# Six pairs of column blocks of an input projection as seven half products each, on token-major operands, with weights loaded two k tiles at a time

## The chip, the core and the metric

The kernel runs on one core of a Trainium2 chip. The metric is the device time of one execution in microseconds (us). TensorE (PE in the profile) does the matrix products, VectorE (DVE) and ScalarE (ACT) the elementwise work, GpSimd (POOL) small powers and the DMAs of its own queue; SyncE (SP) issues most other DMAs. Every engine takes its instructions in the order in which they stand in its queue.

## The reference, cut to what matters

Two layers, 512 tokens, width 2048. `w_in` has 6720 columns:

```python
hn = rms_norm(h, attn_norm[i])
proj = hn @ w_in[i]
(a_u, a_v, a_z, b_b, b_c, b_h, b_z, c_q, c_kv, c_kr, c_z) = jnp.split(proj, split_pts, axis=-1)
y_a = spatial_gating(a_u, a_v, a_z, ...)      # 3 x 512 columns
y_b = short_conv(b_b, b_c, b_h, b_z, ...)     # 4 x 512 columns; c * h goes through a 3-tap conv
y_c = latent_attention(c_q, c_kv, c_kr, c_z)  # 8 x 192, 512, 64, 1024 columns
h = h + concat(rms_norm(y_a), rms_norm(y_b), rms_norm(y_c)) @ w_out[i]
gate = sigmoid(rms_norm(h, ple_norm[i]) @ w_ple_gate[i])
h = h + gate * (p[i] @ w_ple_proj[i])
```

## The kernel before

All arithmetic is fp32, made of fp32r products. `split` cuts a tile into `hi` (a cast on ACT) and `lo` (source minus `hi`, on DVE), and `mm3` makes three matmuls of each product: hi by hi, hi by lo, lo by hi. Activations are split once and stay on the chip (`splitU`, tiles of the pool `big`); weights come 256 KB at a time: `weight` has SP load a tile `raw` of 128x512 (5 buffers), ACT writes `whi`, DVE writes `wlo` (6 buffers each). One such tile serves 12 matmuls.

`groupT` makes an output with features on partitions: the stationary operand is a 128x128 piece of the weight, the moving one 512 tokens of one k tile of x. `groupN` makes an output with tokens on partitions: the stationary operand is a 128x128 piece of x, the moving one a weight row of 384, 448 or 512 columns. `groupK` is `groupT` with k outermost. All walk the 16 k tiles of x (`xs`).

One layer: `groupK` for `ckv`; `groupT` for `za`, `groupN` for `v`, `groupT` for `u`, the spatial gate; then `c`, `h`, `zb`, `b` by `groupT` with the four query pairs (`queries`, `groupN`) between them; `normed` writes the finished halves of `y` to DRAM. Then attention over 8 heads: `kv` (256-column matmuls), `scores`, softmax, `weightsT` (transposes on PE), `values`. Between these, `fillers` gives PE pieces of independent work (12 matmuls each, counted by `ST` and `FN`): the 8 blocks of `zc`, then the first half of the output projection. At the end the second half of the output projection (`ev_out`) and the gate (`ev_gate`), with six PSUM banks in rotation (`TAGS`).

The framework orders each engine's instructions by the order of the code, by when its own estimate has the operands ready, and by free buffers; the program that results is fixed. Names: `raw`, `whi`, `wlo` are the weight tiles, `hi`, `lo` halves of activations, `mm`, `s`, `o`, `tr` PSUM banks, `rs` the result of `rpow` (a power on POOL), `rT` a row of per-token factors that goes through DRAM (`rd`).

Of the kernel before, what the change touches and what calls it, by code (L numbers as in the profile page):

```python
# [11 lines left out]
F32 = mybir.dt.float32  # L12
# [6 lines left out]
P = 128  # L19
# [24 lines left out]
FQ = 2 * (NOPE + ROPE)  # L44

# [22 lines left out]
NU, RAWB, HIB, SB = 62, 5, 6, 3  # L68

ST, FN = (4, 4, 4, 4, 4), (2, 1, 1, 1, 1)  # L70

FETCH = ((0, 1, 2, 3), (4, 5, 6, 7), (), ())
# [13 lines left out]
def trunk(ctx, tc, xT, pT, pos, freq, pars, rows, wsp, wckv, wv, w512, wq0, wq, wkv, wout, wgate, wple, outT):  # L86
# [6 lines left out]
    wst = ctx.enter_context(tc.tile_pool(name="wst", bufs=4))  # L93
    tmp = ctx.enter_context(tc.tile_pool(name="tmp", bufs=4))
# [13 lines left out]
    TMPS = {"t": 2, "n": 2, "q": 2, "z": 2, "o": 2, "q4": 3}  # L108

    def T(s, tag="t", dt=F32):  # L110
        return tmp.tile([P, S], dt, tag=tag, name=nm(s), bufs=TMPS[tag])

    NB = ("s", "s", "s", "o") if SB == 3 else ("s", "s", "tr", "o")
    BANKS = {"mm": 2, "s": SB, "o": 1, "tr": 5 - SB}
# [6 lines left out]

    ident = cst.tile([P, P], F32, name="ident")
    make_identity(nc, ident)
    ones = cst.tile([P, P], F32, name="ones")
# [9 lines left out]
    ydram = drp.tile([8, 2, P, S], F32, name="ydram")  # L134
    mdram = drp.tile([KD, P, S], F32, name="mdram")
    qdram = drp.tile([HEADS, P, S], F32, name="qdram")
    rdram = drp.tile([NPAIR, P, S], F32, name="rdram")
    zdram = drp.tile([HEADS, P, S], F32, name="zdram")
# [17 lines left out]
    def weight(src, n):  # L156
        raw = wst.tile([P, S], F32, tag="raw", name=nm("raw"), bufs=RAWB)
        sync.dma_start(raw[:, :n], src)
        hi = wst.tile([P, S], F32R, tag="whi", name=nm("whi"), bufs=HIB)
        lo = wst.tile([P, S], F32R, tag="wlo", name=nm("wlo"), bufs=HIB)  # L160
        split(raw[:, :n], None, hi[:, :n], lo[:, :n])
        return hi, lo

    def mm3(out, lh, ll, rh, rl, start, stop):
        pe.matmul(out, lh, rh, start=start, stop=False)  # L165
        pe.matmul(out, lh, rl, start=False, stop=False)  # L166
        pe.matmul(out, ll, rh, start=False, stop=stop)  # L167

    def groupT(srcs, xs, evac, tags=("mm",)):

        nq = len(xs) // 4
        for f in range(len(srcs)):
            ps = bank(tags[f % len(tags)])
            for q in range(nq):
                wh, wl = weight(srcs[f][q], S)
                for i in range(4):
                    c = slice(i * P, (i + 1) * P)
                    k = 4 * q + i
                    mm3(ps, wh[:, c], wl[:, c], xs[k][0], xs[k][1], k == 0, k == len(xs) - 1)
            evac(f, ps)  # L180

    def groupK(srcs, load, evac):

        pb = [bank(t) for t in NB]
        for i, src in enumerate(srcs):
            xh, xl = load(i)
            wh, wl = weight(src, S)
            for f in range(4):
                c = slice(f * P, (f + 1) * P)
                mm3(pb[f], wh[:, c], wl[:, c], xh, xl, i == 0, i == len(srcs) - 1)  # L190
        for f in range(4):
            evac(f, pb[f])

    def groupN(srcs, xs, n, evac):

        pb = [bank(t) for t in NB]
        for i, (src, (xh, xl)) in enumerate(zip(srcs, xs)):
            wh, wl = weight(src, n)
            for t in range(NT):
                c = slice(t * P, (t + 1) * P)  # L200
                mm3(pb[t][:, :n], xh[:, c], xl[:, c], wh[:, :n], wl[:, :n], i == 0, i == len(xs) - 1)
        for t in range(NT):
            evac(t, pb[t][:, :n])

    class Stat:


        def __init__(self, tag="q"):
            self.acc = None
            self.tag = tag  # L210

        def add(self, src):
            if self.acc is None:
                self.acc = tmp.tile([P, S], F32, tag="acc", name=nm("acc"), bufs=2)
                a.activation(out=self.acc, in_=src, func=AF.Square)
            else:
                sq = T("sq", self.tag)
                a.activation(out=sq, in_=src, func=AF.Square)
                v.tensor_tensor(out=self.acc, in0=self.acc, in1=sq, op=ALU.add)
# [10 lines left out]
    def rpow(m, n):  # L230
        r = small(n, "rs")
        g.tensor_tensor(out=r, in0=m, in1=mhalf[:, 0:n], op=ALU.pow)  # L232
        return r

# [7 lines left out]


    def tables():
# [24 lines left out]
        for unit, bits, n in ((2.0 ** 16, 9, 4), (2.0 ** 2, 11, 2)):  # L269
            piece = rnd(ang, unit, "piece")  # L270
# [4 lines left out]
            for c in cs + [rest]:  # L275
                q = w("q")
# [9 lines left out]
        v.tensor_tensor(out=turn, in0=turn, in1=r, op=ALU.subtract)  # L286

# [5 lines left out]
        for c in cs + [rest]:  # L293
            v.scalar_tensor_tensor(out=turn, in0=k, scalar=-8.0 * c, in1=turn, op0=ALU.mult, op1=ALU.add)
        lim = 3.1415925
# [8 lines left out]
        return cos, sin  # L304
# [37 lines left out]


    st = Stat()
    xs = []
    col = lambda i, c: par[:, i * NCOL + c:i * NCOL + c + 1]

    def load0(k):
        t = T("x")
        a.dma_start(t, xT[k])  # L350
        xs.append(splitU(t, col(0, C_ATTN + k)))
        st.add(t)
        return xs[k]

    cos = sin = None
# [519 lines left out]
```

## Time and profile before

| | before |
|---|---|
| time, median of 3 runs | 2198.72 us (2198.12 to 2202.12) |
| the profiled execution | 2199.84 us, its span 2198.1 us |
| PE busy in the span | 2180.6 us, 10720 matmuls |
| DVE, ACT, POOL busy | 1119.8, 905.0, 221.0 us |
| mean granted TensorE clock | 0.998 |

The profile is of one execution; its time lies 1.7 us above its span and 1.1 us above the median. A busy time of PE counts matmuls that overlap, so what one matmul costs is read as the distance between the starts of neighbours.

### The profile page before, as it was taken

What the parts mean: (1) busy time and instruction counts of PE and PEld (TensorE: products, weight loads), DVE (VectorE), ACT (ScalarE), POOL (GpSimd) and SP (SyncE); (2) the same over time, 40 slices, a digit from 0 to 9 for tenths busy, and PEclk for the clock granted to TensorE, in tenths of its full rate; (3) what the DMA queues carried; (4) which work ended last, traced back from release to release, by engine and by line L of the source; (5) the groups of instructions that cost most, each with busy time, mean ns of one, the idle gap of its engine ahead of it and who ended that gap; (6) DMA issues with size and microseconds to landing.
All of it is one profiled execution on the core that took longest, in us unless ns stands there. A gap on an engine that the chain in (4) does not pass through costs nothing.

```text
span 2198.1 us, 29729 instructions
## 1 busy us (share of the span) xinstructions
PE 2180.6 (99%) x10720; PEld 1872.6 (85%) x10720; DVE 1119.8 (51%) x2326; ACT 905.0 (41%) x1709; POOL 221.0 (10%) x333
## 2 busy tenths in 40 slices
PE   8999999999999999999999999999999999999999
PEld 7888888988888888888888888889888888888887
DVE  7444354436466656655533444444355566575433
ACT  6332233324576544443332323233246665443222
POOL 0000000002131101100000001000021221011000
PEclk9999999999999999999999999999999999999999
DMA  7333534435354444454333335333353644354432
GB/s 212 103 105 91 138 101 117 113 77 188 106 179 145 132 120 125 127 152 120 115 98 104 99 83 151 97 112 119 78 181 109 187 135 135 111 144 136 124 117 70
DMA packets 142740, 272.22 MB, mean 124 GB/s; under 512 B 17329, under 2 KB 34113, under 8 KB 142593
## 3 DMA queue, kind: packets, MB, share of 16 engines
q1 hardware_dynamic: 122256, 214.83, 34.2%
q0 software_dynamic: 18032, 51.30, 7.7%
q10 hardware_dynamic: 2304, 4.20, 0.7%
q8 instruction: 84, 1.38, 0.3%
q14 instruction: 64, 0.52, 0.1%
HBM read 234.58 MB, written 35.67 MB: 123 GB/s over the span
## 4 chain that ended last, share of the span: by engine, by line
PE 74%; DMA 2%; issue 1%; DVE 1%; POOL 0%; ACT 0%; DVEq 0%; ACTq 0%; POOLq 0%
PE mm L165 13%; PE mm L166 13%; PE mm L167 13%; PE s L167 6%; PE s L165 6%; PE s L166 6%; PE o L166 2%; PE o L167 2%; PE o L165 2%; PE tr L639 1%; PE tr L340 1%; PE tr L166 1%; PE tr L167 1%; PE tr L165 1%; PE s L615 1%
## 5 line engine op out<-in xcount | busy, mean ns | idle before, releaser
L145 DVE TENSOR_TENSOR wlo<-raw,whi 128x512 fp32r<-128x512 f32 (+2 forms) x754 | 502.6, 670 | 619.6 <-ACT whi L144 602.5
L144 ACT CAST whi<-raw 128x512 fp32r<-128x512 f32 (+2 forms) x754 | 449.1, 603 | 847.0 <-PE mm L166 426.4
L165 PE MATMUL mm<-hi,whi 128*128 128x512 f32 x1312 | 512.7, 391 | 1.1 <-DVE pt L387 1.0
L166 PE MATMUL mm<-lo,whi 128*128 128x512 f32 x1312 | 511.3, 390 | 0.0
L167 PE MATMUL mm<-hi,wlo 128*128 128x512 f32 x1312 | 511.2, 390 | 0.0
L165 PEld LDWEIGHTS mm<-hi,whi 128*128 128x128 f32 x1312 | 246.4, 188 | 52.0 <-DVE pt L387 1.2
L167 PEld LDWEIGHTS mm<-hi,wlo 128*128 128x128 f32 x1312 | 246.3, 188 | 51.6
L166 PEld LDWEIGHTS mm<-lo,whi 128*128 128x128 f32 x1312 | 246.4, 188 | 49.8
L165 PE MATMUL s<-hi,whi 128*128 128x512 f32 x480 | 184.5, 391 | 5.9 <-ACT whi L144 5.7
L166 PE MATMUL s<-lo,whi 128*128 128x512 f32 x480 | 187.7, 391 | 0.9 <-DVE lo L148 0.9
L167 PE MATMUL s<-hi,wlo 128*128 128x512 f32 x480 | 186.8, 391 | 0.0
L166 PE MATMUL s<-wlo,hi 128*128 128x384 f32 (+2 forms) x480 | 170.2, 355 | 4.7 <-DVE wlo L145 4.7
L167 PE MATMUL s<-whi,lo 128*128 128x384 f32 (+2 forms) x480 | 169.7, 354 | 0.0
L165 PE MATMUL s<-whi,hi 128*128 128x384 f32 (+2 forms) x480 | 169.5, 353 | 0.0
L232 POOL TENSOR_TENSOR rs<-ms,mhalf 128x1 f32<-128x1 f32 (+2 forms) x104 | 89.2, 862 | 733.0 <-DVE ms L405 564.2
L165 PEld LDWEIGHTS s<-hi,whi 128*128 128x128 f32 x480 | 90.4, 189 | 25.2 <-ACT whi L144 5.7
L166 PEld LDWEIGHTS s<-lo,whi 128*128 128x128 f32 x480 | 90.5, 189 | 20.0 <-DVE lo L148 1.4
L167 PEld LDWEIGHTS s<-hi,wlo 128*128 128x128 f32 x480 | 90.5, 189 | 18.7
L165 PE MATMUL mm<-yh,whi 128*128 128x512 f32 x256 | 101.5, 396 | 0.0
L167 PE MATMUL mm<-yh,wlo 128*128 128x512 f32 x256 | 100.3, 392 | 0.0
L166 PEld LDWEIGHTS s<-wlo,hi 128*128 128x128 f32 x480 | 90.8, 189 | 10.9 <-DVE wlo L145 5.4
L166 PE MATMUL mm<-yl,whi 128*128 128x512 f32 x256 | 100.1, 391 | 0.0
(232 smaller groups left out, 3194.7 us busy)
## 6 DMA issues: line engine op xcount, KB each, us to landing
raw<-in_w_dram SPq DMA_DIRECT2D x256, 256.0 KB, 2.7
raw<-in_wout_dram SPq DMA_DIRECT2D x128, 256.0 KB, 2.7
raw<-in_wgate_dram SPq DMA_DIRECT2D x128, 256.0 KB, 2.6
raw<-in_wq_dram SPq DMA_DIRECT2D x96, 192.0 KB, 2.3
raw<-in_wckv_dram SPq DMA_DIRECT2D x32, 256.0 KB, 2.9
raw<-in_wv_dram SPq DMA_DIRECT2D x32, 256.0 KB, 2.6
raw<-in_wkv_dram SPq DMA_DIRECT2D x32, 256.0 KB, 2.8
mdram<-old SPq DMA_DIRECT2D x32, 256.0 KB, 2.0
```

The costliest lines, as they stand in the source:

```text
L144: a.copy(hi, src)
L145: v.tensor_tensor(out=lo, in0=src, in1=hi.bitcast(F32), op=ALU.subtract)
L165: pe.matmul(out, lh, rh, start=start, stop=False)
L166: pe.matmul(out, lh, rl, start=False, stop=False)
L167: pe.matmul(out, ll, rh, start=False, stop=stop)
L232: g.tensor_tensor(out=r, in0=m, in1=mhalf[:, 0:n], op=ALU.pow)
L340: pe.transpose(ps[:, t * P:(t + 1) * P], src(t), ident)
L615: pe.matmul(ps, ql[:, o], kh, start=False, stop=False)
L639: pe.transpose(ps[:, j * HS + i * P:j * HS + (i + 1) * P], pn[i][:, c], ident)
```

## The change

Blocks `c` and `h` now share one walk over k, with tokens on partitions and all eight banks. The other blocks of the projection go in six pairs through `pair`: b with zb, u with za, v with ckv, q0 with q1 (416 columns each, the shared rotary key cut in two), q2 with q3 (384 columns), and the two halves of zc. Of a pair, x is cut into token halves and k halves, the two weights into k halves, and the eight products of a quarter of x by a half of a weight are replaced by seven (Strassen, Winograd's form): `A11`, `A12`, `A22` of x and four sums `S1` to `S4` that `combine` makes once a layer (x is fetched again for it); sums of weights are made on DVE in the fp32 tiles (`add`). Each product is a chain over 4 double k tiles. The pieces are put together from PSUM in 512-wide scaled copies (`copied`, `plus`), and results go to DRAM (`to`, `spill`). What follows a block in its branch (`task_b`, `task_a`, `task_k`, `task_y`) fetches it back, transposes on PE where features are wanted on partitions, and is called in steps, one after each product. `qload` now does the norms of q, and `qside` transposes `z`.

Weight tiles are two k tiles wide (128x1024, 512 KB): 3 buffers of `raw`, 3 each of `whi` and `wlo`, 4 of `R`, which holds the first weight of a pair while sums are made in it. The fillers of attention are now the first half of the output projection alone.

```diff
-NU, RAWB, HIB, SB = 62, 5, 6, 3
-ST, FN = (4, 4, 4, 4, 4), (2, 1, 1, 1, 1)
+NU = 60
+ST, FN = (2, 2, 2, 1, 1), (1, 1, 0, 1, 0)
...
+    def wtile(s, tag, dt=F32):
+        return wst.tile([P, W2], dt, tag=tag, name=nm(s), bufs=4 if tag == "R" else 3)
...
+        def pair(b0, b1, n, out, step):
...
+            def product(bk, name, w, kk, first=False):
+                wh, wl = w
+                for i in range(2):
+                    for t in range(2):
+                        ah, al = X.get(name, 2 * kk + i, t)
+                        c = slice(i * n, (i + 1) * n)
+                        mm3(bk[t][:, :n], ah, al, wh[:, c], wl[:, c], first and kk + i == 0,
+                            kk == KK - 1 and i == 1, skip_group_check=True)
+                step()
...
+            for kk in range(KK):
+                R.append(load(ld0, kk, "R"))
+                raw = load(ld1, kk)
+                product(bx, "A11", pr(R[kk]), kk, True)
+                add(R[kk], raw)
+                if kk == 1:
+                    bw = [bank(t) for t in tw]
+                if kk:
+                    product(bw, "S1", pr(R[kk - 1]), kk - 1, True)
+            c1 = copied(bx, "e1", rN, 0)
+            product(bw, "S1", pr(R[KK - 1]), KK - 1, True)
+            c5 = copied(bw, "e5", rM, 2)
...
+            for kk in range(KK):
+                raw = load(ld1, kk + KK)
+                ra = load(ld1, kk)
+                product(bw, "S4", pr(raw), kk)
+                add(R[kk], raw)
+                add(ra, raw)
+                product(by, "S3", pr(ra), kk, True)
+                if kk:
+                    product(bx, "S2", pr(R[kk - 1]), kk - 1)
...
+            for kk in range(KK):
+                raw = load(ld0, kk + KK)
+                product(by, "A12", pr(raw), kk, True)
+                add(R[kk], raw)
+                if kk:
+                    product(bx, "A22", pr(R[kk - 1]), kk - 1)
...
+        tasks.append(combos((6, 7)))
+        pair(ft(I_B), ft(I_ZB), 512, to((bd, 512), (zbd, 512)), step)
+        drain()
+        tasks.append(task_b())
+        pair(ft(I_U), ft(I_ZA), 512, to((ud, 512), (zad, 512)), step)
...
+        pair(rowsof((wv[L], 0, 512)), rowsof((wckv[L], 0, 512)), 512, out_v, step)
+        drain()
+        tasks.append(task_a())
...
+        tasks.extend((iter([None] * 7), task_k(), task_y()))
+        pair(ft(I_ZC0), ft(I_ZC1), 512, to((zcd[0], 512), (zcd[1], 512)), step)
...
-            src = tw(I_ZC0) + tw(I_ZC1)
-            for f in range(8):
-                ps = bank("mm")
```

How PE's queue reads in a query block before (out, moving operand, stationary operand, shape; three matmuls per product, token tile by token tile):

```order
L165 MATMUL s_2795<-whi_2800,hi_105 128x384
L166 MATMUL s_2795<-wlo_2801,hi_105 128x384
L167 MATMUL s_2795<-whi_2800,lo_106 128x384
L165 MATMUL s_2796<-whi_2800,hi_105 128x384
L166 MATMUL s_2796<-wlo_2801,hi_105 128x384
```

And in the first pair of layer 0, where the first product of phase 1 (`S1`, bank s_975) gives way to those of phase 2:

```order
L172 MATMUL s_975<-whi_1070,lo_970 128x512
L170 MATMUL s_1090<-whi_1114,hi_359 128x512
L170 MATMUL o_1091<-whi_1114,hi_359 128x512
L171 MATMUL s_1090<-wlo_1115,hi_359 128x512
L172 MATMUL s_1090<-whi_1114,lo_360 128x512
L171 MATMUL o_1091<-wlo_1115,hi_359 128x512
L172 MATMUL o_1091<-whi_1114,lo_360 128x512
```

What moved: a weight tile now meets two token tiles for each of its two k tiles, still 12 matmuls, and `S3` (s_1090, o_1091) stands ahead of `S4`, whose banks are being copied.

DVE's queue in the part of attention where before the `zc` fillers ran (`wlo` is the second half of a split, `pt` an eviction, the rest is the norm of a head's keys):

```order
L387 TENSOR_TENSOR pt_4667<-mm_4594,rT_572 128x512
L145 TENSOR_TENSOR wlo_4776<-raw_4773,whi_4775 128x512
L145 TENSOR_TENSOR wlo_4810<-raw_4807,whi_4809 128x512
L403 TENSOR_REDUCE ms_4698<-sq_4696 128x1
L148 SCALAR_TENSOR_TENSOR kvl_4519<-mm_4671,skv_586,kvh_4518 128x128
```

And in phase 2 of the second pair of the change, u with za, where `task_b` runs (L490 is `add`, L601, L605, L608 and L611 are `task_b`):

```order
L140 TENSOR_TENSOR wlo_1669<-raw_1664,whi_1668 128x1024
L601 SCALAR_TENSOR_TENSOR yb_1731<-tr_1726,par,yb_1731 128x511
L608 TENSOR_TENSOR b_1733<-b_1733,zb_1685 128x512
L605 SCALAR_TENSOR_TENSOR yb_1731<-tr_1726,par,yb_1731 128x511
L140 TENSOR_TENSOR wlo_1691<-raw_1666,whi_1690 128x1024
L490 TENSOR_TENSOR raw_1708<-raw_1708,raw_1706 128x1024
L611 TENSOR_TENSOR yb_1731<-yb_1731,tr_1811 128x512
L140 TENSOR_TENSOR wlo_1711<-raw_1706,whi_1710 128x1024
```

What moved: adds and the branch's steps now stand between the splits that PE waits for, and each split is twice as wide.

## Rows read from the trace of the kernel before

**Rows 1.** The page, busy time of the span: engine, us (share), instructions
```profile
PE 2180.6 (99%) x10720; PEld 1872.6 (85%) x10720; DVE 1119.8 (51%) x2326; ACT 905.0 (41%) x1709; POOL 221.0 (10%) x333
```
**Rows 2.** Waits of PE: engine line <- releaser: us in total, times, longest
```profile
PE s L165 <- ACT whi L144: 5.7, 1, 5.7
PE s L166 <- DVE wlo L145: 4.7, 2, 2.4
```
**Rows 3.** Timeline of PE (start us, us), neighbours of each shape at full clock
```profile
99.68 0.39 PE L165 MATMUL s<-whi,hi 128*128 128x512 f32 x1
...
105.80 0.39 PE L165 MATMUL s<-whi,hi 128*128 128x512 f32 x1
...
249.75 0.36 PE L165 MATMUL s<-whi,hi 128*128 128x448 f32 x1
...
252.99 0.36 PE L166 MATMUL s<-wlo,hi 128*128 128x448 f32 x1
...
324.69 0.33 PE L167 MATMUL s<-whi,lo 128*128 128x384 f32 x1
...
327.47 0.33 PE L165 MATMUL s<-whi,hi 128*128 128x384 f32 x1
...
512.05 0.28 PE L166 MATMUL mm<-wlo,hi 128*128 128x256 f32 x1
...
513.00 0.28 PE L165 MATMUL mm<-whi,hi 128*128 128x256 f32 x1
...
580.11 1.03 PE L639 MATMUL tr<-ident,e 128*128 128x128 f32 x8
580.90 0.47 PE L613 MATMUL s<-hi,hi 128*128 128x512 f32 x1
...
53.19 0.95 PE L225 MATMUL tr<-ones,acc 128*128 128x1 f32 x8
```
**Rows 4.** Timeline of PE around the longest wait inside the kernel (idle before)
```profile
498.28 0.69 PE L166 MATMUL s<-wlo,hi 128*128 128x384 f32 x1 [2.33 <-DVE wlo L145]
...
501.00 0.52 PE L165 MATMUL o<-whi,hi 128*128 128x384 f32 x1
```
**Rows 5.** Groups by shape on DVE and ACT: xcount | busy us, mean ns | idle before
```profile
L145 DVE TENSOR_TENSOR wlo<-raw,whi 128x512 fp32r<-128x512 f32 x626 | 430.1, 690 | 491.2 <-ACT whi L144 474.1 <-PE tr L340 6.8 <-PE s L166 3.0
L144 ACT CAST whi<-raw 128x512 fp32r<-128x512 f32 x626 | 383.1, 619 | 677.4 <-PE mm L166 348.0 <-PE o L167 113.5 <-PE s L166 103.6
L145 DVE TENSOR_TENSOR wlo<-raw,whi 128x384 fp32r<-128x384 f32 x96 | 53.3, 556 | 108.4 <-ACT whi L144 108.4
L144 ACT CAST whi<-raw 128x384 fp32r<-128x384 f32 x96 | 48.9, 512 | 142.3 <-PE o L167 69.0 <-PE mm L166 67.9 <-issue 5.2
L148 DVE SCALAR_TENSOR_TENSOR lo<-h,par,hi 128x512 fp32r<-128x512 f32 x48 | 35.9, 751 | 13.0 <-ACT hi L147 13.0
```
**Rows 6.** Windows: stretch, us, busy of PE, PEld, DVE, ACT, POOL, clock, DMA share, GB/s
```profile
110.00:145.00 35.00, 35.00 (x156) 28.97 (x155) 11.85 (x20) 10.59 (x17) 0.91 (x1) 1.00 0.33 98
305.00:336.00 31.00, 31.00 (x163) 28.74 (x162) 12.82 (x22) 8.14 (x16) 0.00 (x0) 1.00 0.30 87
660.00:770.00 110.00, 110.00 (x647) 96.72 (x646) 74.48 (x189) 63.88 (x139) 21.21 (x33) 1.00 0.45 138
```
**Rows 7.** Timeline in attention: the last matmul of a score tile, and its softmax's end
```profile
680.61 0.39 PE L617 MATMUL s<-krl,q 128*128 128x512 f32 x1
...
685.91 1.34 ACT L625 ACTIVATE e<-e,rc 128x512 f32<-128x512 f32 x2
```
**Rows 8.** DMA issues by line: engine, count, KB each, median us to landing
```profile
raw<-in_w_dram SPq DMA_DIRECT2D x256, 256.0 KB, 2.7
...
hdram<-h POOLq DMA_DIRECT2D x16, 256.0 KB, 2.6
...
rd<-rs POOLq DMA_DIRECT2D x10, 2.0 KB, 9.4
```
**Rows 9.** POOL's powers: duration ns min/median/max
```profile
L232 POOL TENSOR_TENSOR rs<-ms,mhalf x104: 537/983/1482, 144.1 to 1860.2; 128x1 f32<-128x1 f32 x64, 128x4 f32<-128x4 f32 x32, 128x5 f32<-128x5 f32 x8
```

More of the change, by code (lines that the diff above doesn't have):

```diff
@@ L154, in splitU @@
         return hi, lo
[L156 to L161, printed above, removed]
-        return hi, lo
[L164 to L203, printed above, removed]
+    def wtile(s, tag, dt=F32):
+        return wst.tile([P, W2], dt, tag=tag, name=nm(s), bufs=4 if tag == "R" else 3)
@@ new lines, in parts, with weight @@
+    def parts(raw, n, ft=False, tags=("whi", "wlo")):
+        hi, lo = wtile("whi", tags[0], F32R), wtile("wlo", tags[1], F32R)
+        if ft:
+            i, o = "p (f i c) -> p i f c", "p (i f c) -> p i f c"
+            split(raw.rearrange(i, f=4, i=2), None, hi.rearrange(o, f=4, i=2), lo.rearrange(o, f=4, i=2))
+        else:
+            split(raw[:, :n], None, hi[:, :n], lo[:, :n])
+        return hi, lo
+    def weight(load, n=2 * S, ft=False, tags=("whi", "wlo")):
+        raw = wtile("raw", "raw")
+        load(raw)
+        return parts(raw, n, ft, tags)
@@ L241, in tokrow, with blocks, scaled, tables @@
         return rt
-    def tables():
+    def blocks(t, n=4):
+        return t.rearrange("p (b c) -> p b c", b=n)
+    def scaled(x, r, n):
+        x3 = blocks(x, n)
+        v.tensor_tensor(out=x3, in0=x3, in1=r.unsqueeze(2).to_broadcast(list(x3.shape)), op=ALU.mult)
+    def tables(res):
         W = NT * HALF
@@ new lines, in trunk @@
+        cs = []
+        for t in range(NT):
+            c = U("c")
+            a.copy(c, pb["c", t])
+            cs.append(c)
+        rN = lay.tile([P, NT], F32, tag="rN", name=nm("rN"))
+        rpow(st.mean(D), NT, rN)
+        rM = lay.tile([P, NT], F32, tag="rM", name=nm("rM"))
+        v.tensor_scalar(out=rM, in0=rN, scalar1=-1.0, scalar2=None, op0=ALU.mult)
+        r2 = small(NT, "r2")
+        v.tensor_tensor(out=r2, in0=rN, in1=rN, op=ALU.mult)
+        chd = spill("chd")
+        for t in range(NT):
+            v.scalar_tensor_tensor(out=cs[t], in0=pb["h", t], scalar=r2[:, t:t + 1], in1=cs[t],
+                                   op0=ALU.mult, op1=ALU.mult)
+            g.dma_start(chd[t], cs[t])
@@ new lines, in trunk, with step, to, out @@
+        tasks = []
+        def step():
+            while tasks:
+                try:
+                    next(tasks[0])
+                    return
+                except StopIteration:
+                    tasks.pop(0)
+        def to(*sps):
+            def out(j, t, x):
+                sp, n = sps[j]
+                g.dma_start(sp[t][:, :n], x[:, :n])
+            return out
+        def combos(ks):
+            for k in ks:
+                X.combine(k, src, L)
+                yield
@@ new lines, in trunk, with out_v @@
+        ssk = lay.tile([P, NT], F32, tag="ssk", name=nm("ssk"))
+        def out_v(j, t, x):
+            if j == 1:
+                sq = U("sq")
+                a.activation(out=sq, in_=x, func=AF.Square, accum_out=ssk[:, t:t + 1])
+                g.dma_start(ckd[t], x)
+                return
+            sq = U("sq")
+            a.activation(out=sq, in_=x, func=AF.Square)
+            m = small(4, "ms")
+            v.tensor_reduce(out=m, in_=blocks(sq), axis=AX.X, op=ALU.add)
+            r = rroot(m, 4, P)
+            v.tensor_tensor(out=x, in0=x, in1=row[:, R_SGU:R_SGU + 512], op=ALU.mult)
+            scaled(x, r, 4)
+            g.dma_start(vd[t], x)
```

580 lines of the change are left out of this document (364 added, 216 removed).

## The prediction

> **What bounds the kernel now.** The page's busy times come first: PE is busy 99% of the span, DVE 51%, ACT 41% [rows 1]. The table of PE's waits says what the last per cent is: 5.7 us at the start, until the first weight is there, and two waits of together 4.7 us on a weight's `lo` half [rows 2]; the rest is gaps too short for that table. So the time is the number of matmuls by what each costs, and only what removes PE work or makes PE wait counts.
>
> What a matmul costs I read from the timeline as the distance between starts of neighbours, since the durations overlap. 28 matmuls of 512 columns in a row, the first and last shown, give (105.80 − 99.68)/27 = 0.2267 us; 448 columns (252.99 − 249.75)/16 = 0.2025; 384 columns (327.47 − 324.69)/16 = 0.1738; 256 columns (513.00 − 512.05)/8 = 0.119; eight transposes take 0.79 us, 0.10 each, and with the switch to and from them I take 0.11; the means' 128x1 matmuls come to about 0.2 each [rows 3]. For 416 columns, which the kernel before lacks, I estimate 0.188, halfway between 384 and 448.
>
> Each of the two inner waits costs more than its 2.3 us. Behind the wait at 498.28 the next eight starts lie (501.00 − 498.28)/8 = 0.34 us apart instead of 0.174, an excess of 1.4 us [rows 4]: a doubled spacing, which is what the lower of the clock's two levels (1.2 GHz for 2.4) makes of it after PE stood still. So a long wait is about 3.7 us, two of them 7.5. There DVE's queue stood on the work of `normed`.
>
> **PE's work.** Counting the matmuls of both programs by shape: 512 columns go from 7448 to 7040, 384 from 1152 to 672, 448 from 384 to none, 416 from none to 672, 256 from 1152 to 1200, transposes from 488 to 648 (what was made with features on partitions now has to be turned), 128x1 from 48 to 32. So −408 × 0.2267 = −92.5, −480 × 0.1738 = −83.4, −384 × 0.2025 = −77.8, +672 × 0.188 = +126.3, +48 × 0.119 = +5.7, +160 × 0.11 = +17.6 and −16 × 0.2 = −3.2: **−107.3 us**. That is certain as far as PE stays fed; it is counted in the program as scheduled, so that the change doesn't do what it says is excluded. With `normed` and its queue gone both long waits go too: **−7.5 us**.
>
> **Can DVE and ACT keep up in the pairs?** Before, a split's subtraction takes 690 ns for 512 columns and 556 for 384, a cast 619 and 512; both are 1.05 and 0.84 ns a column on top of a fixed part [rows 5]. Extended, a 1024-wide subtraction or add is 0.690 + 512 × 0.00105 = 1.226 us, a cast 1.047 (estimates). A 512-wide pair asks of DVE 28 subtractions and 16 sums of weights, 44 × 1.226 = 53.9 us, and some ten shorter operations near the 751 ns of a scaled one [rows 5], 7.4: 61.3 us, against PE's 28 products × 12 matmuls × 0.2267 = 76.2. ACT's 28 casts and its copies come to some 35. In the pair u with za `task_b` adds 20 operations of about 0.7 us, 14 us, to make some 75.5 on DVE, against 76.2 + 32 × 0.11 = 79.7 on PE. So DVE goes from the 34 to 41% of the steady stretches before, 11.85 of 35.0 us and 12.82 of 31.0 [rows 6], to 80 to 95% by summed durations: near, not over. The price is in the cover. A split has to be ready when PE has used up the one ahead. Walking PE's queue from the matmul that frees a `whi` buffer to the first that needs its next tenant, less a cast and a subtraction, the PE work in between has a median of 12.3 us and a least of 7.7 before; with three buffers the median is 3.2, and 58 of 533 places have under 1 us, nearly all in pairs, the tightest where the spatial gate's weight takes one of the three. In the order, one add or step of a branch stands ahead of such a split. What does a place cost? The trace of before has no split this close: the bounds are nothing, and one 1.2 us operation that is still running. Many of the 58 share a cause, and DVE's starts can follow more closely than durations add up; I take 0.4 for 56 of them, **+22 us**, with ends of 0 and 67.
>
> **Attention.** PE's work of a head falls from 32.5 to 24.8 us, since `zc` left the fillers. The softmax from the last score matmul (680.61) to the end of its scaling (685.91 + 1.34) takes 6.6 us [rows 7]. PE work between scores and the transposes that need them had a median of 12.0 and a least of 7.0 before; now 10.0 and 4.8, two of 64 places under 6 us and some 20 under 8.6, where a softmax that meets a busy ACT or DVE is late. In the stretch from 660 to 770 us DVE was busy 74.5 of 110 us and ACT 63.9 [rows 6]; by the counts of a head both come to three quarters and more. I take **+6 us**, with ends of 0 (all covered) and 25 (20 places × 1.2 us).
>
> **Small terms.** The first weight is 512 KB and its cast 1.047 instead of 0.619 us, and the first wait ends on it: **+2**, between 0.4 (the cast) and 4. At changes of layer and bank sets, and of the first pair whose last two sums are made late: **+3**, 0 to 5.
>
> **At nothing: the transfers.** The raw weight traffic is no more per matmul; 512-column blocks move at 98 GB/s with a DMA share of 0.33, three quarters as long pieces at 87 and 0.30, both about 290 per full share [rows 6]. Even with sums (a weight half is loaded twice for `S3`) and spills a pair asks for some 140 GB/s, half. A spilled result comes back through DRAM: the nearest rows are 2.6 us for a 256 KB store and 9.4 us for a column of 4-byte pieces [rows 8]; `task_b` has two steps, 5.4 us, between a fetch and its transposes. The fetched pieces are 512 bytes long, so nearer to the first: nothing, with the other end below.
>
> **Sum.** 2199.84 (the profiled execution) − 107.3 − 7.5 + 22 + 6 + 2 + 3 = 2118.0; the execution lay 1.1 us above the median, so **2117 us**.
>
> **Rivals.** *The cover holds everywhere*: DVE's queue runs ahead, no place under 1 us shows. Then only the small terms and a little attention stay: about 2090, 2085 to 2097. For it: DVE and ACT are not the bound by sums. Against: 58 places with no slack, and one idle engine cannot catch up across a buffer that isn't free.
>
> *Three buffers are too few throughout the pairs*: DVE's splits wait for a buffer, PE for the split, each product in turn. Of the 336 products (28 in each of 12 pairs) each loses 0.2 us (one 1.2 us operation in six), 67 instead of 22: 2162, 2145 to 2190. For it: three double tiles hold no more than six single ones, yet come free half as often, so that an operation in the way lasts longer against what lies ahead, and the adds stand in the way; against: the median of 3.2 us.
>
> *Slower than before*: PE stands at transposes for spilled data. `task_b` (`ch`, `b`) and `task_k` (`ck`) put 12 such groups a layer into PE's queue, 24 in all, and everything behind one waits. If each fetch took the 9.4 us of the longest landing against a cover of 5.4, PE would stand 4.0 us at a group, 24 × 4.0 = 96 us more: 2213. It decides from a landing of about 8.8 us (24 × 3.4 = 82, the whole gain). Against: the pieces are a hundred times longer than those that took 9.4.
>
> *POOL holds DVE up*: POOL's powers take 537 to 1482 ns, median 983, for tiles of one to five columns [rows 9], a spread far over what the sizes explain; the three forms are mixed in it, so it may or may not show a wait for another engine. POOL's arithmetic goes from 116 to 148 instructions. If each of the 32 held a split back by its own median, at a place without slack, the sum would be 32 × 0.98 = 31 us more: 2149. The Trainium skill, "SBUF — State Buffer", section "SBUF: two separate sides", says that a DVE operation with two SBUF inputs and a GpSimd operation that reads SBUF take a shared pair of ports for the whole instruction and block each other. It speaks against this change, whose sums of weights and subtractions are all of that kind and twice as long; the spread agrees with it, but no row here shows one waiting for the other.
>
> **How the numbers follow.** Forecast (PE-bound, some cover lost, 2097 to 2145) 0.55; cover holds 0.17; three buffers late throughout 0.15; POOL 0.06; slower 0.05; within 0.2% 0.02. 0.2%, some 4 us, is about what a measurement of this kernel can tell from no change. The range leaves out the slower case, no change and the outer parts of two others: 2088 to 2165. Faster 0.93, same 0.02, slower 0.05.
>
> **What would show it.** PE's busy time near 2090 us, and the spacings of 0.227 and 0.174 again in the pairs: the first term. Waits of PE on `wlo` and `whi` of together 20 to 30 us, in pieces under 1.5 us, in the pairs and most in u with za and q0 with q1: the second; at 60 and more the third rival, and near none the first. DVE's share in the pairs 75 to 95%, ACT's near half. In attention PE's transposes waiting for ACT's scaling, some 6 us. The two long waits on `wlo` gone. Waits of PE's transposes on a DMA of several us, 12 a layer: the slower rival. What would make it wrong: a clock at its lower level in the pairs, where every short stall costs more than itself, or a 1024-wide operation that takes much more than 1.23 us.

## The result, and the profile after

The changed kernel takes 2235.42 to 2240.71 us where the kernel before takes 2198.09 to 2202.12: a ratio of 1.0178 (95% interval 1.0157 to 1.0198). 2117 us was forecast. The profiled execution took 2240.71 us, its span is 2238.9. A fourth execution, at a mean granted clock of 0.847, took 2366.20 us and is left out.

The busy times, as in [rows 1], and some of PE's waits, the longest first, as in [rows 2], both of the changed kernel (PEld is the loading of stationary operands):

```profile
PE 2121.8 (95%) x10296; PEld 1796.2 (80%) x10296; DVE 1485.6 (66%) x2246; ACT 1071.0 (48%) x1625; POOL 355.6 (16%) x541
```

```profile
PE mm L171 <- DVE wlo L140: 23.5, 13, 6.0
PE s L171 <- DVE wlo L140: 21.1, 22, 4.7
PE mm L170 <- ACT whi L139: 15.3, 9, 7.9
PE mm L170 <- ACT kn L803: 7.0, 2, 4.9
...
PE tr L330 <- DMA ch<-chd: 3.8, 2, 1.9
PE tr L330 <- DMA ck<-ckd: 3.6, 3, 1.4
```

PE has 424 records fewer, and is idle for 117 us of the span instead of 17.5. The mean granted clock fell from 0.998 to 0.987. The gain was made and more than given back.

Where? I cut PE's row of starts into stages and take from each stage its matmuls at the spacings of [rows 3] (and 0.188 us for 416 columns). What is left over of the stage's time is called lost below; low clock is in it. In us:

| lost | before | changed | 16-byte rows | and 4 KB pieces |
|---|---|---|---|---|
| projection (both layers) | 14.5 | 102.4 | 74.6 | 57.1 |
| attention (both layers) | 10.2 | 50.6 | 48.5 | 48.6 |
| output projection, gate | 0.8 | 20.5 | 3.9 | 3.8 |
| sum | 25.5 | 173.5 | 127.0 | 109.5 |

The last two columns are experiments below. The matmuls themselves come to 2161.9 us before and 2053.1 after, 108.8 less. PE's first wait is 7.9 us for 5.7. The granted clock was at its lower level in 14 stretches of 3.4 or 6.8 us instead of two (and at the very end in both); what it cost against full clock, half of each stretch, adds up to 31 us instead of 4.4.

One stall shows how it happens. First the chain of waits of the changed kernel where the second pair, u with za, gives way to the third, v with ckv (start, us, what), then VectorE and PE in the timeline:

```profile
264.66 0.99 DVE wlo L140
...
266.55 1.14 DVE raw L490
267.71 10.16 DMA raw<-in_wckv_dram
...
279.10 1.23 DVE raw L490
```

```profile
277.96 2.36 DVE L490 TENSOR_TENSOR raw<-raw,raw 128x1024 f32<-128x1024 f32 x2 [6.59 <-DMA raw<-in_wckv_dram]
280.24 2.35 DVE L140 TENSOR_TENSOR wlo<-raw,whi 128x1024 fp32r<-128x1024 f32 x2
```

```profile
276.98 0.61 PE L170 MATMUL mm<-whi,hi 128*128 128x512 f32 x2
281.51 0.80 PE L171 MATMUL mm<-wlo,hi 128*128 128x512 f32 x1 [3.92 <-DVE wlo L140]
282.11 0.63 PE L172 MATMUL mm<-whi,lo 128*128 128x512 f32 x1
282.53 0.63 PE L171 MATMUL mm<-wlo,hi 128*128 128x512 f32 x1
```

Read it backwards. PE waits 3.92 us for a split. The table of waits blames VectorE, but VectorE stood still for 6.59 us at the head of its queue: at a sum of weights (L490) whose weight landed 10.16 us after its issue, and that load had been issued at 267.71, behind the sum at 266.55, once a buffer of `raw` was free. Behind the wait PE's starts are 0.42 us apart and more instead of 0.2267, the spacing of the lower clock.

Why 10 us? The same place by windows of 4 us (us, then the busy us and the number of instructions of PE, PEld, DVE, ACT and POOL, then clock, DMA share, GB/s):

```profile
262.00:266.00 4.00, 4.00 (x19) 3.32 (x18) 3.48 (x4) 1.05 (x1) 2.60 (x3) 1.00 0.71 229
266.00:270.00 4.00, 4.00 (x20) 3.30 (x19) 3.48 (x4) 2.00 (x2) 0.55 (x1) 1.00 1.44 209
270.00:274.00 4.00, 4.00 (x19) 3.33 (x18) 1.23 (x1) 1.17 (x2) 0.00 (x0) 1.00 0.69 25
274.00:278.00 4.00, 3.59 (x16) 2.63 (x14) 0.04 (x1) 1.05 (x1) 0.98 (x2) 1.00 0.43 76
```

From 270 to 274 us the DMA engines are as busy as from 262 to 266 (a share of 0.69 and 0.71) and move 25 GB/s instead of 229. At 264.11 POOL had issued `rd<-rs`, the 2 KB of per-token factors in 512 pieces of 4 bytes; it landed after 12.6 us, and the two loads and the store issued in the 4 us behind it after 10.1 to 10.9.

### The profile page after: what moved, and what is told of

Read it like the earlier page. It is cut to its first block, busy times and chain, and to the rows that moved or that the text cites. A ratio compares the mean times of both kernels' runs of the same rounds, so it can differ in the third digit from the quotient of the medians.

```text
span 2238.9 us, 27910 instructions
## 1 busy us (share of the span) xinstructions
PE 2121.8 (95%) x10296; PEld 1796.2 (80%) x10296; DVE 1485.6 (66%) x2246; ACT 1071.0 (48%) x1625; POOL 355.6 (16%) x541
## 4 chain that ended last, share of the span: by engine, by line
PE 53%; DMA 20%; DVE 14%; issue 9%; ACT 3%; POOL 1%; SPq 1%; DVEq 0%; POOLq 0%; ACTq 0%
PE mm L171 8%; PE mm L172 8%; PE mm L170 8%; DMA raw<-in_w_dram 6%; DVE wlo L140 6%; PE s L171 6%; PE s L172 6%; PE s L170 5%; DMA raw<-in_wq_dram 4%; DVE raw L490 3%; DMA raw<-in_wckv_dram 2%; PE o L171 2%; PE o L172 2%; PE o L170 2%; PE tr L170 1%
## 5 line engine op out<-in xcount | busy, mean ns | idle before, releaser
L139 ACT CAST whi<-raw 128x1024 fp32r<-128x1024 f32 (+3 forms) x536 | 527.1, 987 | 697.3 <-PE mm L172 126.6
L140 DVE TENSOR_TENSOR wlo<-raw,whi 128x1024 fp32r<-128x1024 f32 (+3 forms) x536 | 607.5, 1143 | 219.8 <-ACT whi L139 218.8
L490 DVE TENSOR_TENSOR raw<-raw,raw 128x1024 f32<-128x1024 f32 (+2 forms) x192 | 219.3, 1145 | 164.3 <-DMA raw<-in_w_dram 69.4
L171 PE MATMUL s<-wlo,hi 128*128 128x512 f32 (+2 forms) x624 | 239.6, 384 | 21.1 <-DVE wlo L140 20.8
L171 PE MATMUL mm<-wlo,hi 128*128 128x512 f32 (+3 forms) x672 | 235.5, 350 | 23.5 <-DVE wlo L140 23.5
L172 PE MATMUL s<-whi,lo 128*128 128x512 f32 (+2 forms) x624 | 235.4, 377 | 0.0
L172 PE MATMUL mm<-whi,lo 128*128 128x512 f32 (+3 forms) x672 | 233.0, 347 | 0.0
L170 PE MATMUL mm<-hi,whi 128*128 128x512 f32 x544 | 217.7, 400 | 11.5 <-DVE h L998 5.2
L170 PE MATMUL s<-whi,hi 128*128 128x512 f32 (+2 forms) x624 | 222.4, 380 | 4.9 <-ACT whi L139 4.9
L172 PE MATMUL mm<-hi,wlo 128*128 128x512 f32 x544 | 215.3, 396 | 1.8 <-DVE wlo L140 1.8
L171 PE MATMUL mm<-lo,whi 128*128 128x512 f32 x544 | 215.5, 396 | 0.0
L171 PEld LDWEIGHTS s<-wlo,hi 128*128 128x128 f32 x624 | 118.0, 189 | 48.5 <-DVE wlo L140 32.1
```

What stands on the lines that cost most here:

```text
L139: a.copy(hi, src)
L140: v.tensor_tensor(out=lo, in0=src, in1=hi.bitcast(F32), op=ALU.subtract)
L170: pe.matmul(out, lh, rh, start=start, stop=False, **kw)
L171: pe.matmul(out, lh, rl, start=False, stop=False, **kw)
L172: pe.matmul(out, ll, rh, start=False, stop=stop, **kw)
L490: v.tensor_tensor(out=x[:, :n2], in0=x[:, :n2], in1=y[:, :n2], op=ALU.add)
```

## Experiments

### The store of the per-token rows

Theory A1: this store holds up all transfers. Edit (`x1_row16`, and the same in the kernel before as `y1_before16`); the order of every engine is unchanged in both, so that nothing but the store and the strided reading of its row differs:

```diff
-        g.dma_start(rd.rearrange("(t p) -> p t", p=P), r)
+        g.dma_start(rd.rearrange("(p t) -> p t", p=P), r)
...
-        return rt
+        return rt.rearrange("p (c t) -> p t c", t=NT)
```

> The per-token factors go to DRAM in 128 pieces of 16 bytes instead of 512 pieces of 4 bytes; rows are read with a stride instead, all else as in the changed kernel (2239 us). Theory A1: the four longest stalls in the pairs (4.9, 4.1, 6.2 and 4.1 us) come about because every transfer issued beside such a store takes some 10 us; with the store a few us long they go, and with them the low clock behind them and part of the wait for the row in the output projection and the gate: 2195 to 2215 us. Rival: at those places too many weight loads are issued at once, and the store suffers with them: 2233 to 2245 us, landings there still 9 us and more.

> The kernel before with its ten per-token rows stored in 16-byte pieces; the order of every engine is that of the kernel before. Theory A1 says that these stores slowed every transfer there too, but that five 256 KB loads and six split tiles ahead hid nearly all of it: only the two waits of 2.3 us with their low clock can go, 2190 to 2198 us. If the stores had cost the kernel before as much as they cost the changed one, it would be near 2150 us.

`x1_row16`: 2193.87 us, with the kernel before at 2202.57 beside it. The store lands after 3.9 instead of 10.5 us (below: changed kernel, then this one, from the table of DMAs), and the load at the place above after 4.52 (from the chain of waits):

```profile
rd<-rs POOLq DMA_DIRECT2D x8, 2.0 KB, 10.5
```

```profile
rd<-rs POOLq DMA_DIRECT2D x8, 2.0 KB, 3.9
```

```profile
265.00 4.52 DMA raw<-in_wckv_dram
```

The pair v with ckv of layer 0 shows what it does to a stage, changed kernel and then `x1_row16` (windows):

```profile
266.10:351.10 85.00, 80.46 (x338) 64.81 (x337) 58.62 (x58) 37.79 (x46) 7.56 (x12) 0.96 0.50 133
```

```profile
263.40:342.00 78.60, 77.17 (x337) 62.79 (x336) 58.44 (x58) 37.82 (x46) 7.46 (x12) 1.00 0.46 144
```

So eight small stores cost 46 us: 28 in the projection, 17 in the output projection and the gate, 2 in attention. About half of it was the clock, whose cost went from 31 to 9 us. A1 holds. What makes such a store hold the others up is not shown. `y1_before16` came to 2189.76 us (ratio to the kernel before 0.9959, 0.9944 to 0.9974): ten such stores cost the kernel before 9 us, and the two waits of [rows 2] on `wlo` are gone with `normed` still in place; the longest wait behind the first is now

```profile
PE s L166 <- DVE lo L148: 1.0, 1, 1.0
```

Of the same disturbance the changed kernel felt five times as much. It has three loads ahead instead of five and three split tiles instead of six, if twice as wide, and it moves more (145 GB/s in the mean for 124). No run changes the number of buffers alone, so that this is the reason is argued and not shown.

### Weights that land late

Theory A2: what is left is the same chain with ordinary landings. Rival D: VectorE lacks time.

```diff
-                               w512[L, gi, :, kk // 2, :, o].rearrange("f p c -> p f c"))
+                sync.dma_start(raw, w512[L, gi, kk])
```

> The changed kernel with the 16-byte store (2194 us), and the weights of the 512-column blocks laid out so that a load is 128 pieces of 4 KB instead of 512 of 1 KB; every engine's order is unchanged. Theory A2 (what is left in the pairs is weights that land late, since a load is issued only when one of three buffers comes free, and VectorE's queue stands at the sum that needs it): landings of these weights fall from 4.9 to some 4 us, the waits on splits in b with zb, u with za and zc shrink, the other pairs stay: 2178 to 2190 us. Rival D (VectorE's own time): landings fall, the time stays at 2190 to 2197 us.

`y5_wide`: 2176.19 us (2168.46 to 2182.00), ratio 0.9895 (0.9866 to 0.9923), so 1% faster than the kernel before. These loads land after 4.0 us instead of 4.8 (`x1_row16`, then this run):

```profile
raw<-in_w_dram SPq DMA_DIRECT2D x152, 512.0 KB, 4.8
```

```profile
raw<-in_w_dram SPq DMA_DIRECT2D x152, 512.0 KB, 4.0
```

Windows of b with zb, q0 with q1 and zc, all of layer 1, `x1_row16` first:

```profile
1187.80:1267.50 79.70, 77.76 (x341) 63.19 (x342) 59.61 (x61) 36.34 (x39) 8.04 (x13) 1.00 0.52 163
1435.00:1510.40 75.40, 68.69 (x365) 64.62 (x364) 61.42 (x82) 39.74 (x69) 22.99 (x31) 1.00 0.63 199
1576.20:1664.30 88.10, 82.34 (x363) 66.37 (x363) 76.19 (x83) 43.05 (x50) 14.41 (x23) 0.98 0.53 165
```

```profile
1179.80:1256.50 76.70, 76.70 (x342) 63.46 (x342) 60.86 (x62) 36.37 (x39) 8.04 (x13) 1.00 0.53 172
1418.70:1498.10 79.40, 69.72 (x366) 66.01 (x364) 61.41 (x83) 39.89 (x69) 23.21 (x31) 0.98 0.61 189
1562.90:1646.30 83.40, 80.59 (x363) 65.41 (x362) 75.86 (x83) 42.97 (x50) 13.50 (x23) 1.00 0.54 168
```

The pairs whose loads were changed gain 3.0 and 4.7 us at the same work of VectorE; q0 with q1, whose loads weren't, is no shorter. b with zb runs without a gap: 76.7 us for 76.2 us of matmuls, with VectorE at 79%. A2 holds for these stages, and for b with zb D falls: VectorE at 60.86 of 76.70 us is no bound once weights land in time. In zc, where VectorE is busy for 75.86 of 83.40 us and 4.4 us stay lost, D is not excluded for what is left.

Three more runs on this gave less.

```diff
-                v.tensor_tensor(out=x[:, :n2], in0=x[:, :n2], in1=y[:, :n2], op=ALU.add)
+                v.tensor_tensor(out=x[:, :n2], in0=x[:, :n2], in1=x[:, :n2], op=ALU.add)
```

> Each sum of weights adds the first tile to itself, so that it takes VectorE the same time but doesn't wait for the landing of the second tile (the sums are wrong, and the second tile of phase 1 is read by nothing); all else as in the changed kernel. Theory A2: the stalls at splits behind a sum go for the most part: 2170 to 2200 us. Rival D (it is VectorE's time that lacks): 2230 to 2245 us.

`x4_self`: 2242.53 us, beside 2202.57. The total speaks for D, the stages against it: v with ckv loses 0.6 and 0.5 us instead of 8.8 and 10.9, zc 4.5 and 3.3 instead of 9.4 and 8.4, though q0 with q1 loses more, 13.2 and 15.8 for 10.9 and 12.0. But the framework, which sees other readers, put the program in another order, and attention, the output projection and the gate lost 19 us more. The run tells nothing of the whole.

```diff
                 add(R[kk], raw)
-                add(ra, raw)
-                product(by, "S3", pr(ra), kk, True)
                 if kk:
                     product(bx, "S2", pr(R[kk - 1]), kk - 1)
+                add(ra, raw)
+                product(by, "S3", pr(ra), kk, True)
```

> The changed kernel with the 16-byte store, and in phase 2 of a pair S2 written ahead of S3, so that the reloaded tile has one product (2.7 us) longer to land before its sum. Theory A2: the stalls of phase 2 shrink, 2180 to 2192 us. Rival D: 2190 to 2200 us.

`y3_swap`: 2212.87 us, beside 2198.67: 19 more than `x1_row16`, spread over the pairs b with zb, u with za, v with ckv and zc, of whose eight stages five saw the low clock instead of two. Both theories missed; what in the new order costs this is not shown.

```diff
-                d = raw[:, :2 * n].rearrange("p (i c) -> p i c", i=2)
...
+                sync.dma_start(raw[:, :w.shape[-1]], w[kk])
```

> As the run with 4 KB pieces for the 512-column blocks (2176 us), and every other weight of 1024, 832 or 768 columns (v, ckv, the queries, both output projections, the gate) also laid out as 128 pieces, one transfer each where q1 had two. Theory A2: landings of these fall from 3.7 to 4.1 to some 3.4 to 3.7 us, v with ckv and q2 with q3 (2.6 to 4.2 us lost each) go to 1 to 2, q0 with q1 (10 and 14 us) loses a third: 2160 to 2172 us. Rival: the stalls left there come from the branch and from the three split buffers: 2172 to 2180 us.

`z1_allwide`: 2176.66 us, ratio 0.9869 (0.9853 to 0.9886), not to be told from `y5_wide`. The pairs stay where they were (v with ckv 2.6 and 4.2 us lost in both). The time is the rival's, but the loads that were changed land after 3.6 to 4.1 us, as before (3.5 to 4.0): pieces of 2 KB were long enough, and what the rest waits for the run doesn't show.

### Sums on GpSimd

```diff
-                v.tensor_tensor(out=x[:, :n2], in0=x[:, :n2], in1=y[:, :n2], op=ALU.add)
+                g.tensor_tensor(out=x[:, :n2], in0=x[:, :n2], in1=y[:, :n2], op=ALU.add)
```

> The sums of weights (192) are made by GpSimd, not VectorE; all else as in the changed kernel. Theory A2 (a sum that waits for its weight holds the splits behind it in VectorE's queue): the splits of other tiles go ahead, and only the split of the sum itself is late; the stalls of the pairs, some 100 us with the low clock, shrink to half or less: 2170 to 2200 us, unless a sum takes GpSimd over 3 us. Rival D (VectorE has too much work in the pairs): 2150 to 2190 us, and the run with sums from resident tiles stays at 2239. Rival P (a sum on GpSimd and VectorE's operations on two SBUF tiles exclude each other): VectorE's 1024-wide operations get up to twice as long and the time stays at 2230 or goes above.

`x3_pool`: 2334.82 us, beside 2202.57. Rival P: a sum takes POOL 1.82 to 4.52 us, and VectorE's subtractions, 1.25 us at most in the changed kernel, now take up to 5.27 (min/median/max in ns, all widths together; changed kernel first):

```profile
L140 DVE TENSOR_TENSOR wlo<-raw,whi x536: 408/1217/1248, 7.9 to 2221.8; 128x1024 fp32r<-128x1024 f32 x134, 128x768 fp32r<-128x768 f32 x19, 128x832 fp32r<-128x832 f32 x17, 128x512 fp32r<-128x512 f32 x5
```

```profile
L140 DVE TENSOR_TENSOR wlo<-raw,whi x536: 409/1224/5266, 7.7 to 2315.6; 128x1024 fp32r<-128x1024 f32 x134, 128x768 fp32r<-128x768 f32 x19, 128x832 fp32r<-128x832 f32 x17, 128x512 fp32r<-128x512 f32 x5
L490 POOL TENSOR_TENSOR raw<-raw,raw x192: 1820/2411/4520, 90.9 to 1756.3; 128x1024 f32<-128x1024 f32 x128, 128x832 f32<-128x832 f32 x32, 128x768 f32<-128x768 f32 x32
```

This is what the Trainium skill, "SBUF — State Buffer", section "SBUF: two separate sides", says of the two engines' shared ports; this trace agrees. In the changed kernel itself the longest subtraction is 1.248 us, so there the rule cost the subtractions nothing. How much of the 95 us that this run is slower than the changed kernel is such waiting, and how much the slower sums, it doesn't tell.

### Branches and buffers in q0 with q1

That pair loses 10.3 and 13.8 us in `y5_wide`. Theory B: ScalarE stands at fetched data. Theory C: the spatial gate's weight takes one of three buffers. For `y4_lead` a further `yield` stands behind the fetches of the three branches (`vn` is fetched with `za`, and in the zc pair `task_k` starts four steps earlier); for `z4_spill` five of the spilled tensors (`ch`, `b`, `zb`, `ckv`, `zc`) have their 128-column blocks outermost; and for `z2_wsp` the gate's weight has tiles of its own:

```diff
-                    wsh, wsl = weight(lambda raw: sync.dma_start(raw[:, 0:HS], wsp[L][:, c]), HS)
+                    wr, wt = U("wr"), U("ws", F32R)
+                    sync.dma_start(wr[:, 0:HS], wsp[L][:, c])
+                    wsh, wsl = wt[:, 0:HS], wt[:, HS:S]
+                    split(wr[:, 0:HS], None, wsh, wsl)
```

and, of `y4_lead` and `z4_spill`, one place each:

```diff
                 fetch(z, zbd, c)
                 yield
                 yield
+                yield
...
-                fetch(x, chd, c)
+                fetchF(x, chd, f)
```

> The changed kernel with the 16-byte store, and in the three branches one step (one product) more between the fetch of spilled data and its first use. Theory B (ScalarE's silu and copies and PE's transposes stand at data that has not come back from DRAM, with casts of weights queued behind them): q0 with q1 loses 4 to 5 us less in each layer, u with za and zc 1 to 2 us: 2175 to 2188 us. Rival: the branches cost by their work, not by their waits: 2190 to 2200 us.

> As the run with 4 KB pieces for the 512-column blocks (2176 us), but the weight of the spatial gate has tiles of its own, so that it takes none of the three buffers of raw, whi and wlo in q0 with q1. Theory C (of my prediction: three buffers, and one of them taken): ScalarE's casts no longer wait 2.6 to 4.4 us for PE in that pair, which loses 4 to 8 us less in each layer: 2160 to 2169 us. Rival B (silu and copies that stand at fetched data): 2172 to 2180 us.

> As the run with 4 KB pieces for the 512-column blocks (2176 us), but ch, b, zb, ckv and zc are spilled in blocks of 128 columns, so that a fetch is 128 pieces of 2 KB instead of 512 of 512 bytes (and the store of a tile 512 pieces of 512 bytes instead of 128). Theory B: the fetches land in some 2.7 instead of 3.6 us, the waits of the transposes on ch and ck go, 2168 to 2175 us. Rival: the smaller pieces of the stores hold the weights up as the 4-byte ones did, in proportion: 2176 to 2190 us.

`y4_lead`: 2206.14 us, beside 2198.67, 12 more than `x1_row16`. The wait for `za` is gone, but the pair loses 14.1 and 11.1 us instead of 10.5 and 9.8: `vn`, fetched with it, now ends a stall of 3.7 us, so that one stand at a fetch took the place of another. `z4_spill`: 2180.57 us, beside 2204.6, no difference from `y5_wide`: `ch` lands after 3.1 instead of 3.5 us, `ck` after 4.1 for 4.3. That speaks against B in u with za and in zc, whose fetches these are; q0 with q1 fetches `u`, `za` and `vn`, which were left as they were. For that pair B stays open.

`z2_wsp`: 2234.35 us, beside 2204.6. Its pair loses 5.3 and 8.4 us instead of 10.3 and 13.8, as C said, and yet the run is no test of C. The program came out in another order: of the gate's 24 matmuls a layer all but one left the pair for zc, and the transposes of the branch with them. The third matmul of the gate's products, first and last start behind the durations, in `y5_wide` (q0 with q1 of layer 0 runs from 338 to 414 us) and then in `z2_wsp` (from 335 to 403):

```profile
L172 PE MATMUL tr<-vh,wlo x16: 278/282/283, 357.4 to 1495.2; 128*128 128x256 f32 x16
```

```profile
L172 PE MATMUL tr<-vh,ws x16: 280/283/283, 472.0 to 1644.7; 128*128 128x256 f32 x16
```

So 10 of the pair's 24 us come with the branch, by its buffer, its work or its fetches, and 14 stay without it. The price stands elsewhere: zc loses 19.5 and 18.3 us instead of 4.6 and 4.4, `task_k` slipped out of it in turn, and attention loses 66 and 60 us. The new tiles come from the pool `big`; that the branch waits there for free ones is likely and not shown. Attention now starts with waits for its fetches and splits:

```profile
PE mm L170 <- ACT hi L142: 36.6, 16, 13.2
PE tr L333 <- DMA ck<-ckd: 18.3, 4, 6.2
```

### Attention

Theory E: too little independent work for PE between the steps of a head. Theory T: ScalarE's table loads, 36 where there were 24, since each head's silu now stands between exponentials. For T, silu moves to the eviction of the zc pair and a copy stays (`x2_silu` on the changed kernel, `w1_silu` on `y5_wide`). For E `z3_fill` does filler work twice, and `w2_start` moves pieces (`w3_both` does that and `w1_silu`):

```diff
                 for q in range(2):
+                    for k in range(4):
+                        c = slice(k * P, (k + 1) * P)
+                        if q == 0:
+                            mm3(ps, w[0][:, c], w[1][:, c], ys[k][0], ys[k][1], k == 0, k == 3)
                     wout_part(f, 0, ps, q, w)
...
-            a.activation(out=sz[h], in_=ps, func=AF.Silu)
+            a.copy(sz[h], ps)
...
-ST, FN = (2, 2, 2, 1, 1), (1, 1, 0, 1, 0)
+ST, FN = (4, 3, 1, 0, 0), (1, 1, 0, 1, 0)
```

> silu of zc is taken when the pair's results are evicted, not in the heads of attention, where a plain copy stays; all else as in the changed kernel. Theory: the 28 table loads of 1.28 us that Silu and Exp force on ScalarE in attention are what makes PE late there (44 us lost against 11 before); nearly all of them go: 2210 to 2225 us. Rival: attention is late since too little independent work stands between its steps, and ScalarE's loads fill time that it would have waited: 2232 to 2245 us.

> As the run with 4 KB pieces for the 512-column blocks (2176 us), but the first half of each filler of attention is done twice on PE from the same split weight (the first result is overwritten): 16 times 12 matmuls a layer, 87 us of PE work more, nothing more on ScalarE, VectorE or the transfers. Theory E (attention loses 28 and 21 us since too little independent PE work lies between its steps): half of these stalls or more go, so 2263 - 25 and below, 2225 to 2240 us. Rival (they are waits at places without a filler, or for transfers): 2252 to 2268 us.

> As the run with 4 KB pieces for the 512-column blocks (2176 us), and silu of zc taken when the pair's results are evicted, with a copy in its place in attention. Theory T (ScalarE's 28 table loads of 1.28 us between Exp and Silu are part of what attention loses, which the first run of this edit could not show beside the stores): attention loses 10 us less in both layers together: 2162 to 2170 us. Theory E alone (cover, wherever the work on ScalarE stands): 2172 to 2182 us.

> As the run with 4 KB pieces for the 512-column blocks (2176 us), but of the eight pieces of independent work ahead of the heads of attention four instead of two stand at the first wait, three at the second, one at the third and none behind. Theory E: the waits for the keys' norm at the start of attention (5.5 us in layer 0, 2.9 in layer 1, and the low clock behind the first) shrink by the 5.4 us that two pieces take, and what is taken away at the end of the start comes back as waits there in part: 2168 to 2175 us. Rival: it comes back in full, 2174 to 2182 us.

> Both edits together. Theories T and E: their gains add, 2155 to 2168 us. E alone: 2168 to 2178 us.

`z3_fill`: 2246.39 us, beside 2204.6. That is 0.0295 of the kernel before more than `y5_wide` by the ratios, 65 us for 87 us of added PE work. Attention by windows, `y5_wide` and then `z3_fill`:

```profile
547.50:819.60 272.10, 255.52 (x1495) 221.04 (x1495) 181.62 (x416) 171.90 (x331) 68.17 (x98) 0.99 0.37 119
1632.00:1897.10 265.10, 254.20 (x1495) 220.86 (x1494) 178.65 (x406) 171.46 (x331) 67.82 (x98) 0.99 0.39 118
```

```profile
553.00:850.00 297.00, 291.56 (x1671) 253.83 (x1670) 182.62 (x417) 172.05 (x333) 69.09 (x98) 0.99 0.36 109
1667.00:1966.00 299.00, 292.26 (x1672) 254.34 (x1671) 179.33 (x406) 172.13 (x331) 69.52 (x98) 0.99 0.34 105
```

176 and 177 more matmuls, 40 us each, lengthen the stretches by 25 and 34 us: some 21 us of the added work filled time that PE had stood. DVE and ACT do the same work in both. The whole lies between the ranges of E and of its rival; in the stage E holds for nearly half: attention loses 27 instead of 49 us.

`x2_silu`: 2247.48 us, beside 2202.57, no gain. `w1_silu`: 2174.35 us, ratio 0.9858 (0.9844 to 0.9873), overlapping that of `y5_wide`; 28 table loads (1.283 us each) are gone, and attention loses 44 instead of 49 us. T is some 4 us by the stage, less than half of what it said; the ratios, 0.9858 for 0.9895, make it 8 us with an error nearly as large. `w2_start`, more pieces at the start and none behind: 2188.56 us, beside 2206.53; attention loses 56. `w3_both`: 2185.42 us, ratio 0.9894 (0.9866 to 0.9922). The waits at the start shrink (for `kn` from 6.4 to 2.9 us in all), and gaps open behind it: moved this way, the cover is missed where it was.

## Why the prediction was wrong, step by step

- **PE's work, −107.3 us: right.** 108.8 by the traces, with spacings as read in [rows 3] and 0.189 for 416 columns (estimate 0.188). A 1024-wide subtraction took 1.220 us in the mean (estimate 1.226) and a cast 1.050 (1.047).
- **"At nothing: the transfers": the step that failed.** It compared bandwidths, 140 GB/s asked of some 290, and a mean rate says nothing of when one tile lands. (That the weight traffic is no more per matmul was wrong too: a pair loads 20 tiles of 512 KB for its 336 matmuls, some 30 KB each, where a tile of 256 KB served 12, 21 KB each; the windows of `x1_row16` above show 144 to 199 GB/s.) Two costs were there. The 4-byte stores: 46 us (`x1_row16`). Their 9.4 us stood in [rows 8], but I took it as the landing of one small store, not as the time that all other transfers take beside it. What the windows above show could have been read in the trace before, behind its first such store at 61.7 us, where loads of 256 KB landed after 7.9 to 10.3 us:

```profile
65.00:69.00 4.00, 4.00 (x19) 3.27 (x19) 0.88 (x5) 1.90 (x2) 0.00 (x0) 1.00 0.14 24
69.00:73.00 4.00, 4.00 (x19) 3.31 (x18) 0.02 (x1) 0.00 (x0) 1.59 (x2) 1.00 0.42 33
```

  The 1 KB pieces cost another 18 us (`y5_wide`). The row at hand was 2.7 us for a 256 KB tile; the 512 KB tile takes 4.9, with three buffers and VectorE's queue standing at the sum.
- **"There DVE's queue stood on the work of `normed`": right, but it stopped there.** Ahead of that wait VectorE stands at `normed`'s first multiplication (L452, L455) for its row `rT`, which comes through such a store (kernel before, then `y1_before16`):

```profile
495.26 2.50 DVE L452 TENSOR_TENSOR yb<-yb,rT 128x512 f32<-128x512 f32 x4 [10.78 <-DMA rT<-rd]
```

```profile
487.88 4.07 DVE L455 TENSOR_TENSOR yb<-yb,rT 128x512 f32<-128x512 f32 x4 [3.18 <-DMA rT<-rd]
```

  `y1_before16` keeps `normed` and is rid of both waits. The change took `normed` away and kept the stores, so the −7.5 us came at these two places and was paid back at others.
- **Split lookahead, +22 us: the place was right, the size was not, and that three buffers are the cause is not shown.** The projection loses 102 us against 14.5 before; 28 go with the stores and 17.5 with the pieces, both of them a matter of when a weight lands. The 57 left are 24 in q0 with q1, 30 in the ten other pairs (0.1 to 4.9 each) and 3 elsewhere. Of the 24, 10 go when the spatial gate's branch leaves the pair (`z2_wsp`); whether its buffer, named in the prediction as the tightest place, costs them is open, and so are the other 14.
- **Attention, +6 us (0 to 25): mis-sized.** It is +40. The median of PE's work between scores and transposes had fallen only from 12.0 to 10.0 us, but it counts one wait of a head; keys, queries and values wait as well, and all of them had lost cover with `zc`. Half of it, 21 us, is shown to be cover (`z3_fill`); the rest is open.
- **The clock, not in the sum.** I charged 1.4 us of low clock to each of two long waits that were to go, and none to new ones. The prediction named a low clock in the pairs among the signs of being wrong, at no price. Fourteen low stretches cost most of 31 us; with the stores mended 9 us are left.
- **Small terms: right as far as measured.** The start came to +2.2 us; the +3 at changes of layer and bank sets was not taken apart.
- **The rivals.** The kernel became slower, but not as the slower rival said: transposes waited for spilled data for 7.4 us in all, not 96. GpSimd held no subtraction up (1.248 us at most). Three late buffers throughout, 67 us, was nearest in place and size; what the runs showed behind it are late landings.

Of the 122.7 us between forecast (2118.0 for the profiled execution) and 2240.7, the stores are 46.8, the pieces 17.7, attention beyond its term 32 (48.6 − 10.2 − 6, with both of these mended), and some 26, their cause open, are what the projection still loses beyond its terms.

## What to carry to other kernels

When a change makes prefetch shallower, bound each transfer by its worst landing in the trace, not by mean bandwidth, and look at what is in flight beside it: a 2 KB store in 4-byte pieces held loads up for some 10 us, and cost 9 us in the kernel with five loads ahead and 46 in the one with three. If PE waits for a split, go on to what the splitting engine itself stood at; an in-order queue passes one late tile on to every tile behind it. A stage whose independent work is taken away pays at every wait of the stage, and work that PE was given only to fill is worth keeping until its cover is counted.

## What the runs showed of the hardware

- A store of 512 pieces of 4 bytes landed after 10.5 us (median of eight, 9.2 to 12.6), and weight loads issued beside it after 7.9 to 12.2, but for one of 3.7; in 128 pieces of 16 bytes it landed after 3.9 (1.7 to 6.3) and the loads beside it after 2.7 to 5.8. The Trainium skill, "DMA: Bandwidth & Descriptors", section "Specifications", says that pieces under 512 bytes don't reach the line rate; 16-byte pieces are under it as well and did no such harm here.
- 512 KB in 1 KB pieces landed after 4.8 us, in 4 KB pieces after 4.0, every engine's order being the same (`x1_row16`, `y5_wide`); between pieces of 2 KB and 4 KB there was no such difference (`z1_allwide`).
- GpSimd's 1024-wide fp32 sum took 2.34 to 4.52 us beside VectorE's work; 1024-wide VectorE subtractions, 1.25 us at most without, took up to 3.87 beside such sums, and 832-wide ones, 1.03 at most, up to 5.27 (`x3_pool`).
- The granted clock fell to its lower level for 3.4 or 6.8 us 14 times in the changed kernel, four times with the stores mended, each time after or while PE stood; not every stand brought it, one of 2.80 us ahead of 152.03 us did not.
